# Making the first chunk's normalised MLP tiles one filler later in a streaming encoder layer

## The chip, the cores and the metric

The kernel runs on one core of a Trainium2 chip. The metric is the device time of one execution in microseconds, the median over several runs. One execution was also recorded by the hardware profiler; its instructions, waits and transfers are the trace that is read below. Engines are named as in the profile: PE (matrix multiplication), DVE (vector engine), ACT (scalar engine), POOL (GpSimd) and SP, whose queue issues most of the transfers.

## The reference

One layer over 1024 prompt frames and 32 sample frames, 1056 columns in all, with a model width of 1024, in float32. What matters here is the order of its parts:

```
x = x + (sigmoid(ga) * (A @ w_attn_out) + sigmoid(gb) * (B @ w_conv_out)) @ w_mix_out
x = x + softmax((rms_norm(x, g_cross) @ w_cq) @ K_mem.T) @ V_mem @ w_co      # 4 heads of 64, 256 memory tokens
x = x + square(relu(rms_norm(x, g_mlp) @ w_up)) @ w_down                     # hidden width 4096
y = rms_norm(x, g_final)
```

`rms_norm` divides a frame by the root of the mean square over its 1024 features and multiplies with a gain per feature.

## The kernel before

**Layout.** Features lie on the 128 partitions in eight blocks (f = 0 to 7), frames along the free axis. The 1056 frames are cut into three chunks of 384, 384 and 288 columns (`CH`, line 23). Every float32 operand of a matmul is split into a high and a low part (`split`, lines 128 to 130: ACT casts, DVE subtracts), and a product is three matmuls, high by high, high by low, low by high (`gemm`, lines 195 to 202). A projection of one weight block is 8 x 3 = 24 matmuls into one accumulator in PSUM. There are three accumulators (`n_acc`, line 103; tag "acc"), used in turn, so a projection can start only when the result three before it has been read out.

**The stage.** The change lies where three chunks overlap: chunk 0 is done with cross-attention and waits for the MLP, chunk 1 goes through cross-attention, and chunk 2 through its trunk, the eight projections of `do_conv_out` and then the eight of `do_mix`. The trunk projections and the first MLP products are the *fillers*: a list of 48 pieces of PE work (lines 1716 to 1723). Fillers 0 to 7 are `do_conv_out(2, f)`, 8 and 9 the first two of `do_mix(2, f)`, 10 is the first MLP product of chunk 0 (`up_one(0, 0)`). Behind each filler the table `at`, filled by `then(i, ...)` (lines 1724 to 1766), hangs further steps:

- at filler 1, `chunk_stats(1)`: chunk 1's scale, summed by small matmuls (L232), a root and a correction step (L238 to L243), spread over 128 partitions by L251 on ACT and L252 on DVE and two matmuls (L253, L254), copied to R by L266;
- at filler 2, `do_cq` twice: chunk 1's queries, each a projection of 24 matmuls of 384 columns, read out by L1142 and split by L1146 (ACT) and L1147 (DVE);
- at fillers 3, 5, 7, 9, 11 and 12, the cross-attention of chunk 1, a unit for each of the four heads, in three parts that are staggered by one step: `scores` (L1173 on PE, then L1176, L1179, L1181 on DVE and L1178 on ACT), `turn` (transposes L1190, split by L129 and L130 into PTh and PTl) and `values` (L1209, read out by L1211, L1212). Scores have one place in PSUM, so the next unit's wait until L1178 has read the last one's;
- at fillers 0 to 3, two a filler, `normed(0, f)` (lines 1316 to 1330): chunk 0's tile f, multiplied with gain and scale by L1318 on DVE, written to DRAM by L1321 on SP's queue, and its first 264 columns split by L1329 on ACT and L1330 on DVE. The split tiles are read by filler 10 (L890 to L892); the written ones are read back at filler 18 (L1265) and later.

`do_conv_out(2, f)` (lines 1070 to 1083) loads a residual part by L1074, runs the 24 matmuls, reads the accumulator out by L1078 on DVE (called the *eviction* of f), adds the residual by L1079 (POOL, for f = 7 DVE) and splits the sum by L129 and L130 into the tiles M. `do_mix(2, f)` reads all eight pairs of M and is read out by L1093.

**What sets the order.** Temporary tiles of DVE's steps and of these loads share one ring of six buffers (`tmp`, tag "ct", lines 29 and 105). The fillers and `at` give the program's order; a scheduler then places the instructions of each engine, but keeps those that are marked with `pin` in program order among themselves. L1318 and L1330 are marked so. On the chip each engine takes its own list strictly in that order, and each instruction waits for its operands and for the buffer that it writes.

## Time and profile before

| | us |
|---|---|
| median of three runs | 1738.01 |
| the three runs | 1736.62, 1738.01, 1741.13 |
| the profiled execution | 1736.25 |
| its span, first to last instruction | 1734.5 |
| PE busy | 1721.6 |
| DVE busy | 1194.1 |
| ACT busy | 852.4 |
| the eight tiles of chunk 0: first and last L1318 | 966.8 to 989.5 |

A row of the timeline gives the start from the span's beginning, the duration, the engine, the line, the operation, the tile written and the tiles read, and the shapes; a bracket at the end gives how long the engine had been idle just before, and what ended the wait. A row of windows gives a stretch, its length, the busy time of the five engines with instruction counts, the clock granted to PE as a share of full speed, the share of the transfer engines and GB/s. The profiler shows matmuls as longer than their spacing, since one begins while the one before drains; the spacing is read from the starts.

### The profile page before, as it was taken

The page shows a single profiled execution, that of the slowest core. Times are in us where ns is not written, and L with a number is a line of the kernel's source. Part 1 is how long each engine was busy: PE and PEld are TensorE (multiplying, and loading weights), DVE is VectorE, ACT ScalarE, POOL GpSimd, SP SyncE. Part 2 cuts the span into 40 slices and gives each one's busy share as a digit, 9 for nine tenths or more (in the row PEclk, how much of TensorE's full clock was granted, in tenths as well). Part 3 has the DMA queues.
Part 4 walks back from the last instruction along what each step waited for, and adds up shares of the span by engine and source line. Part 5 has one row for each costly group of instructions (what it writes and reads, how often), then busy time and mean ns, then how long its engine had stood idle before and what let it go on. Part 6 is the DMA issues. An engine that isn't in the chain of part 4 may idle for free.

```text
span 1734.5 us, 32561 instructions
## 1 busy us (share of the span) xinstructions
PE 1721.6 (99%) x12238; PEld 1707.3 (98%) x12238; DVE 1194.1 (69%) x2279; ACT 852.4 (49%) x1664; POOL 596.2 (34%) x668
## 2 busy tenths in 40 slices
PE   9999999999999999999999999999999999999998
PEld 8999999999999999999999999999999999999998
DVE  7776776867766657556677788787666686545675
ACT  8653533535335324434556666764444563433443
POOL 0026366453643444452225242106555410000121
PEclk9999999999999999999999999999999999999999
DMA  4333344433445888866865667676666695555554
GB/s 187 101 128 121 125 134 136 130 133 131 148 142 197 292 291 282 302 227 227 279 223 197 222 227 257 225 265 208 220 222 215 218 323 181 194 186 173 191 171 161
DMA packets 179853, 346.60 MB, mean 200 GB/s; under 512 B 18656, under 2 KB 101248, under 8 KB 179568
## 3 DMA queue, kind: packets, MB, share of 16 engines
q1 hardware_dynamic: 163504, 290.07, 50.6%
q0 software_dynamic: 15568, 53.68, 8.8%
q8 instruction: 96, 1.57, 0.4%
q10 hardware_dynamic: 624, 0.77, 0.1%
q14 instruction: 61, 0.50, 0.1%
HBM read 250.73 MB, written 93.14 MB: 198 GB/s over the span
## 4 chain that ended last, share of the span: by engine, by line
PE 88%; DMA 5%; DVE 3%; ACT 1%; issue 1%; POOL 1%; SPq 1%; DVEq 0%; ACTq 0%; POOLq 0%
PE acc L200 12%; PE acc L202 12%; PE acc L201 12%; PE acc L890 6%; PE acc L891 6%; PE acc L892 6%; PE acc L1830 5%; PE acc L1829 5%; PE acc L1828 5%; PE pc L890 2%; PE pc L891 2%; PE pc L892 2%; PE pt L607 2%; DVE wl L130 1%; DMA wr<-wsum_d 1%
## 5 line engine op out<-in xcount | busy, mean ns | idle before, releaser
L129 ACT CAST wh<-wr 128x1024 fp32r<-128x1024 f32 (+1 forms) x214 | 223.7, 1046 | 365.3 <-PE acc L1829 114.8
L130 DVE TENSOR_TENSOR wl<-wr,wh 128x1024 fp32r<-128x1024 f32 (+1 forms) x214 | 275.9, 1289 | 105.2 <-ACT wh L129 103.4
L200 PE MATMUL acc<-X,wh 128*128 128x384 f32 (+1 forms) x864 | 281.4, 326 | 0.0
L201 PE MATMUL acc<-X,wh 128*128 128x384 f32 (+1 forms) x864 | 278.5, 322 | 0.0
L202 PE MATMUL acc<-X,wl 128*128 128x384 f32 (+1 forms) x864 | 277.8, 322 | 0.0
L285 POOL TENSOR_TENSOR xacc<-xacc,ct 128x384 f32<-128x384 f32 (+1 forms) x57 | 77.7, 1366 | 380.8 <-ACT ct L283 379.0
L201 PEld LDWEIGHTS acc<-X,wh 128*128 128x128 f32 x864 | 162.7, 188 | 0.7
L200 PEld LDWEIGHTS acc<-X,wh 128*128 128x128 f32 x864 | 162.4, 188 | 0.8
L202 PEld LDWEIGHTS acc<-X,wl 128*128 128x128 f32 x864 | 162.4, 188 | 0.1
L200 PE MATMUL acc<-Y,wh 128*128 128x384 f32 (+1 forms) x432 | 139.8, 324 | 2.2 <-DVE ct L1078 2.2
L202 PE MATMUL acc<-Y,wl 128*128 128x384 f32 (+1 forms) x432 | 139.3, 323 | 0.1
L201 PE MATMUL acc<-Y,wh 128*128 128x384 f32 (+1 forms) x432 | 139.2, 322 | 0.0
L129 ACT CAST PTh<-pt 128x512 fp32r<-128x512 f32 (+3 forms) x94 | 45.8, 517 | 112.1 <-PE pt L607 110.4
L1828 PE MATMUL acc<-n,wh 128*128 128x264 f32 x352 | 100.2, 285 | 0.0
L1829 PE MATMUL acc<-n,wh 128*128 128x264 f32 x352 | 100.1, 284 | 0.0
L1830 PE MATMUL acc<-n,wl 128*128 128x264 f32 x352 | 100.0, 284 | 0.1
L744 POOL TENSOR_TENSOR ws<-ws 128x256 f32<-128x256 f32 x100 | 93.7, 937 | 5.7
L744 POOL TENSOR_TENSOR xacc<-xacc 128x256 f32<-128x256 f32 x100 | 86.5, 865 | 5.8 <-DMA xacc<-in_w_in 0.4
L200 PEld LDWEIGHTS acc<-Y,wh 128*128 128x128 f32 x432 | 81.1, 188 | 3.1 <-DVE ct L1078 3.1
L202 PEld LDWEIGHTS acc<-Y,wl 128*128 128x128 f32 x432 | 81.1, 188 | 0.4 <-DMA wl<-wl_d 0.4
L201 PEld LDWEIGHTS acc<-Y,wh 128*128 128x128 f32 x432 | 81.1, 188 | 0.0
L593 ACT ACTIVATE S<-S,nmx 128x257 f32<-128x257 f32 (+1 forms) x132 | 64.2, 488 | 20.1 <-DVE nmx L588 18.8
(440 smaller groups left out, 5555.3 us busy)
## 6 DMA issues: line engine op xcount, KB each, us to landing
wr<-in_w_up SPq DMA_DIRECT2D x53, 512.0 KB, 4.5
wr<-in_w_in SPq DMA_DIRECT2D x52, 512.0 KB, 3.6
wr<-wsum_d SPq DMA_DIRECT2D x40, 512.0 KB, 3.5
wr<-in_w_conv_out SPq DMA_DIRECT2D x24, 512.0 KB, 3.7
wr<-in_w_mix SPq DMA_DIRECT2D x24, 512.0 KB, 4.5
wr<-in_w_down SPq DMA_DIRECT2D x24, 512.0 KB, 3.6
n_d<-Z SPq DMA_DIRECT2D x32, 264.0 KB, 4.3
xacc<-in_w_down POOLq DMA_DIRECT2D x16, 512.0 KB, 4.6
```

The source lines that it names most:

```text
L129: act.copy(hi, src)
L130: dve.tensor_sub(lo, src, hi.bitcast(F32))
L200: pe.matmul(out, wh[:, a], hi, start=(k == 0), stop=False)
L201: pe.matmul(out, wh[:, a], lo, start=False, stop=False)
L202: pe.matmul(out, wl[:, a], hi, start=False, stop=(k == len(acts) - 1))
L744: pin(pool_e.tensor_tensor(t[:, to], t[:, x], t[:, y], op=ALU.add))
L890: pe.matmul(acc, wh[:, a], hi, start=(start and k == 0), stop=False, skip_group_check=True)
L891: pe.matmul(acc, wh[:, a], lo, start=False, stop=False, skip_group_check=True)
L892: pe.matmul(acc, wl[:, a], hi, start=False, stop=(k == 3), skip_group_check=True)
L1828: pe.matmul(a, wh[:, s], hi, start=(t == 0 and k == 0), stop=False, skip_group_check=True)
L1829: pe.matmul(a, wh[:, s], lo, start=False, stop=False, skip_group_check=True)
L1830: pe.matmul(a, wl[:, s], hi, start=False, stop=(t == 1 and k == 7), skip_group_check=True)
```

## The change

The loop that hangs the eight tiles behind the fillers starts at filler 1 instead of 0:

```
     for f in range(NF):
-        then(f // 2, call(normed, 0, f))
+        then(1 + f // 2, call(normed, 0, f))
```

Two tiles now come behind each of fillers 1 to 4. At filler 1 they stand behind `chunk_stats(1)`, at filler 2 behind the two query projections, at filler 3 ahead of the first scores, as the last two did before; filler 4 had nothing. The operations are the same; what the scheduler makes of them on each engine differs from about filler 1 to the end of the cross-attention of chunk 1.

The first place is DVE at the eviction of f = 1. In these names acc_11275 (after: acc_11261) is the accumulator of f = 1, ct_11253 and ct_11260 are the first two normalised tiles, wl is the low part of a weight. Before:

```order
L252 SCALAR_TENSOR_TENSOR ct_11243<-ident,rc_11225,ct_11242 128x128 x3
L130 TENSOR_TENSOR wl_11393<-wr_2080_11390,wh_11392 128x1024
L238 TENSOR_SCALAR st_v_11312<-pq_11308 128x3
L1318 SCALAR_TENSOR_TENSOR ct_11253<-Ga_1703_9819,prm,R_11240 128x384
L240 RECIPROCAL st_y_11314<-st_s_11313 128x3
L241 TENSOR_TENSOR st_t_11315<-st_v_11312,st_y_11314 128x3
L242 SCALAR_TENSOR_TENSOR st_t_11315<-st_t_11315,st_y_11314 128x3
L1330 TENSOR_TENSOR Y_2044_11257<-ct_11253,Y_2043_11256 128x264
L1318 SCALAR_TENSOR_TENSOR ct_11260<-Ga_1715_9868,prm,R_11240 128x384
L1078 TENSOR_TENSOR ct_11300<-acc_11275,Ga_1385_8179 128x288
```

and after:

```order
L252 SCALAR_TENSOR_TENSOR ct_11243<-ident,rc_11225,ct_11242 128x128
L1078 TENSOR_TENSOR ct_11286<-acc_11261,Ga_1385_8179 128x288
L252 SCALAR_TENSOR_TENSOR ct_11243<-ident,rc_11225,ct_11242 128x128 x2
L130 TENSOR_TENSOR wl_11379<-wr_2074_11376,wh_11378 128x1024
L238 TENSOR_SCALAR st_v_11298<-pq_11294 128x3
```

The eviction has moved from behind the weight split and the first two tiles into the group of L252 that spreads chunk 0's scale.

The second place is DVE at the evictions of f = 4 and f = 5 (acc_11563 and acc_11603 before, acc_11549 and acc_11603 after). S, rec and nmx belong to the softmax of a unit (unit 0: 11543 before and 11529 after; unit 1: 11642, nmx_11643; unit 2: 11757, nmx_11758; unit 3: nmx_11889). Before:

```order
L1179 RECIPROCAL rec_11546<-den_11545 128x3
L1181 TENSOR_SCALAR S_11543<-S_11543,rec_11546 128x256 x3
L130 TENSOR_TENSOR wl_11673<-wr_11670,wh_11672 128x1024
L1330 TENSOR_TENSOR Y_2110_11526<-ct_11522,Y_2109_11525 128x264
L1318 SCALAR_TENSOR_TENSOR ct_11529<-Gb_1786_10160,prm,R_11240 128x384
L1078 TENSOR_TENSOR ct_11588<-acc_11563,Gb_1481_8707 128x288
L1078 TENSOR_TENSOR ct_11628<-acc_11603,Gb_1516_8915 128x288
L1176 TENSOR_REDUCE nmx_11643<-sc_11635 128x3
```

After, the stretch that ends with the eviction of f = 4:

```order
L1176 TENSOR_REDUCE nmx_11643<-sc_11635 128x3
L130 TENSOR_TENSOR M_11505<-ct_11501,M_11504 128x288
L1318 SCALAR_TENSOR_TENSOR ct_11508<-Gb_1752_10017,prm,R_11240 128x384
L130 TENSOR_TENSOR PTl_11659<-pt_11654,PTh_11658 128x384
L130 TENSOR_TENSOR PTl_11667<-pt_11662,PTh_11666 128x384
L1179 RECIPROCAL rec_11645<-den_11644 128x3
L1181 TENSOR_SCALAR S_11642<-S_11642,rec_11645 128x256 x3
L1176 TENSOR_REDUCE nmx_11758<-sc_11750 128x3
L1330 TENSOR_TENSOR Y_2104_11512<-ct_11508,Y_2103_11511 128x264
L1318 SCALAR_TENSOR_TENSOR ct_11515<-Gb_1764_10066,prm,R_11240 128x384
L1078 TENSOR_TENSOR ct_11574<-acc_11549,Gb_1481_8707 128x288
```

and the later one that ends with the eviction of f = 5:

```order
L1181 TENSOR_SCALAR S_11757<-S_11757,rec_11760 128x256 x3
L130 TENSOR_TENSOR M_11578<-ct_11574,M_11577 128x288
L1318 SCALAR_TENSOR_TENSOR ct_11581<-Gb_1775_10113,prm,R_11240 128x384
L1176 TENSOR_REDUCE nmx_11889<-sc_11881 128x3
L130 TENSOR_TENSOR wl_11802<-wr_11799,wh_11801 128x1024
L1330 TENSOR_TENSOR Y_2123_11585<-ct_11581,Y_2122_11584 128x264
L1318 SCALAR_TENSOR_TENSOR ct_11588<-Gb_1786_10160,prm,R_11240 128x384
L1078 TENSOR_TENSOR ct_11628<-acc_11603,Gb_1516_8915 128x288
```

Before, the two evictions follow each other and stand ahead of unit 1's maximum; after, the first stands behind unit 2's maximum and the sixth tile (ct_11515), the second behind unit 3's maximum, a weight split and the last tile (ct_11588).

The third place is PE ahead of the projection f = 7 (acc_11718). pt_11654 and pt_11662 are the transposes of unit 0, pt_11783 and pt_11791 those of unit 1, o_11773 the values of unit 0. Before:

```order
L1173 MATMUL sc_11635<-mkl_9881,Y_2086_11426 128x256
L1190 MATMUL pt_11654<-ident,S_11543 128x128
L1190 MATMUL pt_11662<-ident,S_11543 128x128
L1190 MATMUL pt_11654<-ident,S_11543 128x128
L1190 MATMUL pt_11662<-ident,S_11543 128x128
L1190 MATMUL pt_11654<-ident,S_11543 128x128
L1190 MATMUL pt_11662<-ident,S_11543 128x128
L200 MATMUL acc_11718<-Y_1642_9578,wh_11597 128x288
```

and after:

```order
L1173 MATMUL sc_11750<-mkl_9930,Y_2086_11448 128x256
L1209 MATMUL o_11773<-PTl_11667,mv_10077 128x384
L1190 MATMUL pt_11783<-ident,S_11642 128x128
L1190 MATMUL pt_11791<-ident,S_11642 128x128
L1190 MATMUL pt_11783<-ident,S_11642 128x128
L1190 MATMUL pt_11791<-ident,S_11642 128x128
L1190 MATMUL pt_11783<-ident,S_11642 128x128
L1190 MATMUL pt_11791<-ident,S_11642 128x128
L200 MATMUL acc_11718<-Y_1642_9578,wh_11597 128x288
```

The values of unit 0, the scores of unit 2 and the transposes of unit 1, which stood behind f = 7 before, now stand ahead of it.

## The prediction

> **What bounds the kernel now.** I read the page first, then TensorE's waits, its timeline where those waits fall, and the vector engine's timeline at the same place. The page, and the answer on what PE waits for between 960 and 1040 us:

> ```profile
> span 1734.5 us, 32561 instructions
> PE 1721.6 (99%) x12238; PEld 1707.3 (98%) x12238; DVE 1194.1 (69%) x2279; ACT 852.4 (49%) x1664; POOL 596.2 (34%) x668
> PE acc L200 <- DVE ct L1078: 2.2, 3, 0.8
> ```

> PE is busy for all but 13 us of the span, so an edit that leaves PE's work alone can only remove or add waits of PE. In this stage nearly all of them have one cause: three times a projection cannot start because L1078 has not yet emptied one of the three accumulators. PE's rows at these places:

> ```profile
> 968.21 0.33 PE L202 MATMUL acc<-Y,wl 128*128 128x384 f32 x1
> 969.26 0.44 PE L200 MATMUL acc<-Y,wh 128*128 128x384 f32 x1 [0.72 <-DVE ct L1078]
> ...
> 973.71 0.34 PE L254 MATMUL pr<-ct,ones_r 128*128 128x384 f32 x1
> 974.89 0.40 PE L200 MATMUL acc<-Y,wh 128*128 128x288 f32 x1 [0.85 <-DVE ct L1078]
> ...
> 981.34 0.28 PE L1173 MATMUL sc<-mkh,Y 128*128 128x256 f32 x1
> ...
> 982.05 0.29 PE L200 MATMUL acc<-Y,wh 128*128 128x288 f32 x1
> ...
> 985.23 0.29 PE L200 MATMUL acc<-Y,wh 128*128 128x288 f32 x1
> ...
> 989.12 0.82 PE L1190 MATMUL pt<-ident,S 128*128 128x128 f32 x6
> 990.57 0.40 PE L200 MATMUL acc<-Y,wh 128*128 128x288 f32 x1 [0.63 <-DVE ct L1078]
> ...
> 995.21 0.34 PE L1209 MATMUL o<-PTl,mv 128*128 128x384 f32 x1
> 995.38 0.34 PE L1209 MATMUL o<-PTh,mv 128*128 128x384 f32 x1
> ```

> Matmuls overlap, so I count from start to start. A 384-column matmul takes 0.175 us of PE (4.2 for 24); the first gap is 1.05 - 0.18 = 0.87, the second 1.18 - 0.18 = 1.00, the third 1.45 less 0.66 for six transposes = 0.79; each restart costs 0.1 more. Together 2.97 us: the most that can be won here. A 24-matmul projection of chunk 2 takes 3.18 (982.05 to 985.23), six score matmuls 0.71, a values matmul 0.17.

> Whether DVE has room is in the windows of 1000 to 1020 us (PE, PEld, DVE, ACT, POOL busy; granted clock):

> ```profile
> 1000.00:1010.00 10.00, 10.00 (x81) 9.98 (x80) 9.72 (x21) 9.81 (x26) 3.08 (x3) 1.00 0.67 224
> 1010.00:1020.00 10.00, 10.00 (x79) 10.00 (x78) 9.94 (x18) 7.20 (x12) 4.63 (x4) 1.00 0.49 164
> ```

> DVE is 97 to 99% busy there: what is put later arrives where DVE is full.

> **The change part by part.** No operation is added or removed. I write N0 to N7 for the eight tiles; each is one L1318 and one L1330 on DVE, one L1329 on ACT, one write by L1321. Projection f of chunk 2 is "f0" to "f7", units 0 to 3 are the heads of chunk 1's cross-attention. What goes first: the evictions of f1 and f2 stood behind N0 to N3. DVE before:

> ```profile
> 959.68 0.16 DVE L238 TENSOR_SCALAR st_v<-pq 128x3 f32<-128x3 f32 x1 [0.33 <-PE pq L232]
> ...
> 961.48 0.94 DVE L252 SCALAR_TENSOR_TENSOR ct<-ident,rc,ct 128x128 fp32r<-128x128 f32 x3 [0.60 <-ACT ct L251]
> ...
> 966.38 0.16 DVE L238 TENSOR_SCALAR st_v<-pq 128x3 f32<-128x3 f32 x1 [0.80 <-PE pq L232]
> ...
> 968.23 0.61 DVE L1318 SCALAR_TENSOR_TENSOR ct<-Ga,prm,R 128x384 f32<-128x384 f32 x1
> 968.76 0.45 DVE L1078 TENSOR_TENSOR ct<-acc,Ga 128x288 f32<-128x288 f32 x1
> ...
> 977.97 2.31 DVE L1147 TENSOR_TENSOR Y<-ct,Y 64x384 fp32r<-64x384 f32 x4
> ...
> 980.85 1.22 DVE L130 TENSOR_TENSOR wl<-wr,wh 128x1024 fp32r<-128x1024 f32 x1
> 981.98 0.42 DVE L1330 TENSOR_TENSOR Y<-ct,Y 128x264 fp32r<-128x264 f32 x1
> 982.33 0.61 DVE L1318 SCALAR_TENSOR_TENSOR ct<-Gb,prm,R 128x384 f32<-128x384 f32 x1
> 982.86 0.45 DVE L1078 TENSOR_TENSOR ct<-acc,Gb 128x288 f32<-128x288 f32 x1
> 983.22 0.95 DVE L1176 TENSOR_REDUCE nmx<-sc 128x3 f32<-128x768 f32 x1
> ```

> The eviction of f1 starts at 968.76 without a wait of its own. In the new order it stands inside the first L252 group (about 962), so the first gap goes. Steps of DVE from start to start: weight split 1.13, L1330 0.35, L1318 0.53, L1078 0.36 (0.45 if last), L1176 0.87. To f2's eviction: L238 can start at about 966.2; from it to the end of L252 took 2.74 for chunk 0's scale; with the M split of f1 (0.4) that is 969.3, then N0, split, L1330, N1, eviction = 2.99, so 972.3. PE, not stopped, ends the second query projection and the broadcast at 968.4 + 4.2 + 0.35 = 972.9. The second gap goes too, and f3 starts at 972.9 instead of 974.89: 2.0 us ahead.

> What is added: N2 to N7 now fall among the attention units, and the new order of PE packs the units closer. Further steps:

> ```profile
> 987.05 0.18 DVE L1179 RECIPROCAL rec<-den 128x3 f32<-128x3 f32 x1 [0.38 <-ACT S L1178]
> 987.26 0.88 DVE L1181 TENSOR_SCALAR S<-S,rec 128x256 f32<-128x256 f32 x3
> ...
> 992.45 1.01 DVE L130 TENSOR_TENSOR PTl<-pt,PTh 128x384 fp32r<-128x384 f32 x2
> 993.38 0.44 DVE L1078 TENSOR_TENSOR ct<-acc,Gb 128x288 f32<-128x288 f32 x1
> ...
> 1000.60 0.44 DVE L130 TENSOR_TENSOR M<-ct,M 128x288 fp32r<-128x288 f32 x1
> 1000.97 0.55 DVE L1220 TENSOR_TENSOR Y<-tO,Y 64x384 fp32r<-64x384 f32 x1
> 1001.43 1.01 DVE L130 TENSOR_TENSOR PTl<-pt,PTh 128x384 fp32r<-128x384 f32 x2
> ```
> ```profile
> 985.55 0.47 ACT L1178 ACTIVATE S<-sc,nmx 128x256 f32<-128x256 f32 x1
> ...
> 990.50 0.85 ACT L129 CAST PTh<-pt 128x384 fp32r<-128x384 f32 x2
> ```
> ```profile
> L129 ACT CAST wh<-wr 128x1024 fp32r<-128x1024 f32 (+1 forms) x214 | 223.7, 1046 | 365.3 <-PE acc L1829 114.8
> L1079 POOL TENSOR_TENSOR ct<-ct,ct x7: 800/837/1004, 957.1 to 995.5; 128x288 f32<-128x288 f32 x7
> DMA to landing us min/median/max: 2.3/4.1/5.6
> ...
> L1330 DVE TENSOR_TENSOR Y<-ct,Y x8: 422/430/1035, 967.9 to 991.8; 128x264 fp32r<-128x264 f32 x8
> ```

> The landing time is that of L1074, the load that POOL's add waits for. Walking the new order with these steps (a walk by hand, an estimate from these rows):

> f6 needs f3's eviction. DVE ends the L1147 group at 980.28 as before, now with a weight split inside: 981.4; then N2, L1176 of unit 0, L1330, N3 and the eviction: 0.53 + 0.87 + 0.35 + 0.53 + 0.45, to 984.15. PE is done with f4, unit 0's scores and f5 at 972.9 + 9.54 + 0.71 = 983.15. A wait of 1.0; f6 is 1.1 ahead of its old 985.23.

> Unit 0's values. PE has 19 matmuls of f6, unit 1's scores, unit 0's transposes and only 5 more matmuls (0.66) before them; before, f7's whole 3.18 lay there. The transposes end at 988.1; DVE is at L1176 of unit 1 until 988.4, then M 0.37, N4 0.53, and the low part PTl until 989.85; PE could use it at 988.9: a wait of 1.0. Unit 2's scores then wait for ACT, which casts PTh until 989.1 and needs 3 x 0.47 for unit 1's exponentials: 0.25 more, start 990.5.

> f7 needs f4's eviction. After unit 2's scores, the last values matmul and unit 1's transposes PE is done at 992.05. DVE: L1179 and L1181 until 991.6, L1176 of unit 2 0.87, L1330 0.35, N5 0.53, eviction 0.45: 993.8. A wait of 1.75, where 0.79 stood.

> The first mix projection needs f5's eviction. PE: f7 3.18, unit 3's scores, unit 1's values, unit 2's transposes, done at 999.15. DVE after f4's eviction (step end 993.7): tO sum 0.47 (taken like L1220), PTl 0.93, L1179 0.21, L1330 0.35, L1220 0.46, L1181 0.80: 996.95. Then the M split of f4, which hangs on a load: SP issues it behind a weight load that waits for ACT's cast (991.6), so 992.0 + 4.1, POOL 0.84, ACT 0.43, M at 997.4 to 997.8. Then N6, L1176 of unit 3, weight split, L1330, N7, eviction: 0.53 + 0.87 + 1.13 + 0.35 + 0.53 + 0.45: 1001.65. A wait of 2.5, where none stood; queued behind that M split are all these, and PE waits for the last.

> From there I find none: both mix projections have 15 matmuls (4.0 us) ready, within which DVE ends N7 and f7's eviction (about 1004), and the 8 tiles are read only after them. The eight writes move on SP's queue with the tiles, past weight and residual loads; what reads them back stands at filler 18, after both mix projections and more, so I price the writes at nothing, and what they push back at the late load below.

> Sum: new 1.0 + 1.0 + 0.25 + 1.75 + 2.5 + four restarts of 0.1 = 6.9, less 2.97: **+3.9 us**. The profiled execution took 1736.25 (its span and 1.75 around it), so 1740.2; on the median of the three runs, 1738.01, 1741.9. Ends: +2.2 if DVE ends the L1147 group 1.0 earlier, half of what PE is ahead (f6's wait goes), and the load lands by 2.3 (0.7 less); +6.1 if it lands at 5.6 (1.5 more) and POOL's adds hold up DVE by the 0.6 that separates the median and the longest L1330 (a row of the same view). I take the median row for the load.

> [...] The two windows above show the clock at 1.00 behind waits of up to 1.0. [...]

> **The rivals.** (1) *DVE keeps up*: the gates are met and only the three old waits vanish, 1738.0 - 2.97 = 1735.0, or 1736.0 with the first two alone. For it: the rows above show DVE idle for 0.3 to 0.8 us at a time before, so some of its queue can slide. Against: it must be 1.75 and 2.5 us earlier than the walk at two gates, behind 97% of busy time. 20%.

> (2) *The late load* (the other side): f4's residual load, at its new place on SP, lands late; DVE stands at the M split with N6, N7 and f5's eviction behind it. It passes the bound of 0.3% (5.2 us of 1738.0, about what a measurement of this kernel can tell from no change) when it lands 1.3 us over the median, at 5.4; at 5.6 to 7 us it gives +5.4 to +6.8, up to 1744.8. 12%.

> [...] 3%.

> That the tiles are not moved is excluded by the order; a change elsewhere (a few rows differ after 1040 us) gets 5%.

> **How the numbers follow.** Forecast 60%, at 1741.9 with its own ends 1740.2 to 1744.1; about 7 points of it lie over +5.2. Slower: 7 + 12 + 3 + 1 = 23%. Faster by 5.2 is more than all waits of the stage; 3% for what I do not see. Within 0.3%: 74%. The range goes from 1736.5 (most of rival 1) to 1745.0 (most of rival 2).

> **What would show it.** Right: PE's wait at 969 and 974 gone; new waits of about 1.0 before f6 (L1078), 1.0 at L1209 (L130), 1.75 before f7 and 2.5 before the mix projection (both L1078), in all some 6 us of waits where the row of L1078 has 2.2. Wrong: DVE evicting f4 before 992 or f5 before 999; no wait at L1209; a wait at a matmul that reads the eight tiles; any difference that comes from outside this stage.

## The result, and the profile after

| | before | changed |
|---|---|---|
| median of six runs | 1738.70 us | 1747.39 us |
| lowest to highest | 1736.62 to 1741.13 | 1744.76 to 1751.71 |
| profiled execution, its span | 1736.25, 1734.5 | 1744.76, 1742.9 |

The changed kernel is slower: ratio 1.0055, 95% interval 1.0043 to 1.0067, 8.7 us by the medians, where +3.9 was forecast and 1745.0 was the upper end.

The page's first lines, and the answer on what PE waits for between 960 and 1040 us:

```profile
span 1742.9 us, 32561 instructions
PE 1724.8 (99%) x12238; PEld 1708.3 (98%) x12238; DVE 1191.2 (68%) x2279; ACT 852.9 (49%) x1664; POOL 597.2 (34%) x668
PE acc L200 <- DVE ct L1078: 3.6, 3, 2.1
PE o L1209 <- ACT PTh L129: 1.6, 1, 1.6
PE acc L200 <- DVE Gb L1093: 0.7, 1, 0.7
PE o L1209 <- DVE PTl L130: 0.7, 1, 0.7
```

PE was busy 3.2 us longer although it did the same 12238 matmuls. That is the first sign of something that is no wait. The places, in PE's timeline of the changed kernel:

```profile
973.90 0.40 PE L200 MATMUL acc<-Y,wh 128*128 128x288 f32 x1 [0.50 <-DVE ct L1078]
...
984.41 0.37 PE L200 MATMUL acc<-Y,wh 128*128 128x288 f32 x1
...
990.84 0.44 PE L1209 MATMUL o<-PTh,mv 128*128 128x384 f32 x1 [1.65 <-ACT PTh L129]
991.95 0.69 PE L1209 MATMUL o<-PTl,mv 128*128 128x384 f32 x1 [0.67 <-DVE PTl L130]
...
994.37 1.20 PE L1190 MATMUL pt<-ident,S 128*128 128x128 f32 x6
996.54 0.40 PE L200 MATMUL acc<-Y,wh 128*128 128x288 f32 x1 [0.97 <-DVE ct L1078]
...
1004.19 0.40 PE L200 MATMUL acc<-M,wh 128*128 128x288 f32 x1 [2.14 <-DVE ct L1078]
...
1006.03 0.44 PE L202 MATMUL acc<-M,wl 128*128 128x288 f32 x1
1006.27 0.44 PE L200 MATMUL acc<-M,wh 128*128 128x288 f32 x1
```

The first old wait is gone, a bracket of 0.50 is left of the second, and f3 starts 1.0 ahead of its old place. Then come the waits at unit 0's values (990.84, 991.95), before f7 (996.54) and before the mix projection (1004.19). The last two rows show the other thing: matmuls of 288 columns, 0.133 us apart otherwise, start 0.24 apart; and six transposes at 994.37 take 1.20 where they took 0.82. The granted clock is third from the end in the windows of this kernel:

```profile
988.38:991.79 3.41, 1.25 (x8) 0.76 (x6) 1.84 (x4) 1.81 (x6) 0.79 (x1) 0.99 0.89 265
991.79:995.20 3.41, 3.25 (x14) 3.02 (x15) 2.54 (x8) 2.48 (x7) 0.00 (x0) 0.51 0.55 202
995.20:998.61 3.41, 2.44 (x19) 2.21 (x18) 3.29 (x9) 3.06 (x11) 0.81 (x1) 1.00 0.52 187
...
1001.98:1005.39 3.41, 1.27 (x10) 1.20 (x10) 3.41 (x8) 2.93 (x10) 1.03 (x2) 1.00 0.84 252
1005.39:1008.80 3.41, 3.41 (x16) 3.41 (x16) 3.35 (x10) 1.30 (x4) 0.54 (x1) 0.50 0.51 168
...
```

(The columns: window, its length, busy time and instructions of PE, PEld, DVE, ACT and POOL, granted clock, DMA share, GB/s.) Twice the clock stands at one half for exactly one stretch of 3.41 us, and both times the stretch before held only 8 or 10 matmuls.

Where the time went: counted from start to start, the waits are 0.65 (f3), 0.17 (f6), 1.81 and 0.94 (values), 0.97 (f7, with the slow transposes taken out) and 2.29 (mix), and with 0.1 for each of four restarts 7.2 us (behind the wait at 973.90 the next matmul starts 0.24 later, where others of 288 columns stand 0.13 apart). The half-speed stretches add 3.25 / 2 + 3.41 / 2 = 3.3, an estimate from the granted clock of 0.51 and 0.50. Against the 2.97 of before that is +7.6. Just behind the stage PE waits 0.86 at 1026 and 0.44 at 1041 where it waited 0.34 before: +1.0. Together 8.6, where the spans differ by 8.4. The rest of the program comes out nearly even in sum only. Matmul for matmul, at times of the kernel before, the changed kernel is 0.3 us late at 955, 8.0 at 1015, 9.3 at 1040, 8.0 at 1080, 8.8 at 1160 and 8.5 at the end. It gains 1.3 between 1064 and 1080, where the kernel before has a half-speed stretch (its windows stand further down) and the changed one has none.

This tells where PE's time stood, not what each part would save. The first half-speed stretch is an example. A second profile of the changed kernel (run after_light, below) lacks it; there f7 waits 1.45 instead of 0.97, and the mix projection starts at 1004.06 instead of 1004.19, although f3 started 0.2 later. So that stretch, 1.6 by the sum above, delayed PE by about 0.3 net: without it PE comes earlier and waits for DVE instead.

The cause of the largest new wait stands in the timelines of the other engines. First the kernel before, then the changed one, around the residual load of f3 (L1074):

```profile
981.44 0.32 SPq L1074 DMA_DIRECT2D ct<-m_d  x1
981.82 0.45 SPq L172 DMA_DIRECT2D wl<-wl_d  x1
982.36 0.38 SPq L159 DMA_DIRECT2D wr<-in_w_mix  x1
982.84 0.38 SPq L159 DMA_DIRECT2D wr<-in_w_up  x1
...
984.34 0.84 POOL L1079 TENSOR_TENSOR ct<-ct,ct 128x288 f32<-128x288 f32 x1 [7.36 <-DMA ct<-m_d]
```
```profile
980.40 0.33 SPq L159 DMA_DIRECT2D wr<-in_w_mix  x1
980.82 0.38 SPq L172 DMA_DIRECT2D wl<-wl_d  x1
981.49 0.33 SPq L159 DMA_DIRECT2D wr<-in_w_up  x1
982.18 0.33 SPq L1321 DMA_DIRECT2D xn_d<-ct  x1
982.61 0.39 SPq L1074 DMA_DIRECT2D ct<-m_d  x1
...
989.15 0.79 POOL L1079 TENSOR_TENSOR ct<-ct,ct 128x288 f32<-128x288 f32 x1 [14.05 <-DMA ct<-m_d]
...
989.98 0.43 ACT L129 CAST M<-ct 128x288 fp32r<-128x288 f32 x1 [4.19 <-POOL ct L1079]
990.32 0.85 ACT L129 CAST PTh<-pt 128x384 fp32r<-128x384 f32 x2
991.06 0.49 ACT L1178 ACTIVATE S<-sc,nmx 128x256 f32<-128x256 f32 x1
...
990.44 0.46 DVE L130 TENSOR_TENSOR M<-ct,M 128x288 fp32r<-128x288 f32 x1 [1.57 <-ACT M L129]
```

Before, the load was issued ahead of three weight loads of 512 KB and let POOL start 2.9 us later; now it is issued 1.2 us later, behind three such loads and a write, and POOL starts 6.5 us after the issue. POOL's add waits for it, ACT's M cast waits for the add, and ACT takes its list in order: the PTh cast for unit 0 and the exponentials of unit 1, whose inputs were there at about 988.5 and 988.9, stand behind the M cast, for which ACT is idle 4.19 us. DVE stands the same way at the M split, idle for 1.57.

### The profile page after: what moved, and what is told of

It is laid out like the page before. It is cut to its first block, busy times and chain, and to the rows that moved or that the text cites. A ratio compares the mean times of both kernels' runs of the same rounds, so it can differ in the third digit from the quotient of the medians.

```text
span 1742.9 us, 32561 instructions
## 1 busy us (share of the span) xinstructions
PE 1724.8 (99%) x12238; PEld 1708.3 (98%) x12238; DVE 1191.2 (68%) x2279; ACT 852.9 (49%) x1664; POOL 597.2 (34%) x668
## 3 DMA queue, kind: packets, MB, share of 16 engines
q8 instruction: 96, 1.57, 0.4%
## 4 chain that ended last, share of the span: by engine, by line
PE 88%; DMA 5%; DVE 3%; ACT 2%; issue 1%; POOL 1%; SPq 0%; DVEq 0%; POOLq 0%; ACTq 0%
PE acc L200 12%; PE acc L202 12%; PE acc L201 12%; PE acc L890 6%; PE acc L891 6%; PE acc L892 6%; PE acc L1828 6%; PE acc L1830 6%; PE acc L1829 6%; PE pc L890 2%; PE pc L891 2%; PE pc L892 2%; PE pt L607 2%; DMA ct<-m_d 2%; DVE wl L130 1%
## 5 line engine op out<-in xcount | busy, mean ns | idle before, releaser
L129 ACT CAST wh<-wr 128x1024 fp32r<-128x1024 f32 (+1 forms) x214 | 223.7, 1046 | 367.4 <-PE acc L1829 124.3
L130 DVE TENSOR_TENSOR wl<-wr,wh 128x1024 fp32r<-128x1024 f32 (+1 forms) x214 | 276.8, 1294 | 108.3 <-ACT wh L129 107.3
L200 PE MATMUL acc<-X,wh 128*128 128x384 f32 (+1 forms) x864 | 281.4, 326 | 0.0
L202 PE MATMUL acc<-X,wl 128*128 128x384 f32 (+1 forms) x864 | 277.8, 322 | 0.0
L200 PEld LDWEIGHTS acc<-X,wh 128*128 128x128 f32 x864 | 162.4, 188 | 0.8
L202 PEld LDWEIGHTS acc<-X,wl 128*128 128x128 f32 x864 | 162.4, 188 | 0.1
L200 PE MATMUL acc<-Y,wh 128*128 128x384 f32 (+1 forms) x432 | 139.6, 324 | 1.5 <-DVE ct L1078 1.5
L202 PE MATMUL acc<-Y,wl 128*128 128x384 f32 (+1 forms) x432 | 139.2, 323 | 0.5 <-DMA wl<-wl_d 0.5
L129 ACT CAST PTh<-pt 128x512 fp32r<-128x512 f32 (+3 forms) x94 | 45.8, 518 | 113.1 <-PE pt L607 110.6
L1829 PE MATMUL acc<-n,wh 128*128 128x264 f32 x352 | 100.1, 284 | 0.0
L200 PEld LDWEIGHTS acc<-Y,wh 128*128 128x128 f32 x432 | 81.0, 188 | 2.2 <-DVE ct L1078 2.0
L202 PEld LDWEIGHTS acc<-Y,wl 128*128 128x128 f32 x432 | 81.1, 188 | 0.8 <-DMA wl<-wl_d 0.8
```

What stands on the lines that cost most here:

```text
L129: act.copy(hi, src)
L130: dve.tensor_sub(lo, src, hi.bitcast(F32))
L200: pe.matmul(out, wh[:, a], hi, start=(k == 0), stop=False)
L202: pe.matmul(out, wl[:, a], hi, start=False, stop=(k == len(acts) - 1))
L1829: pe.matmul(a, wh[:, s], lo, start=False, stop=False, skip_group_check=True)
```

## The experiments

My theory after reading this (theory 1 below): residual loads that land late hold ACT's and DVE's queues at the M split, PE waits for what is queued behind, and a stretch in which PE stood long enough costs half a stretch more. The rival (theory 2): DVE has too much to do, whatever the loads do. Ratios are to the kernel before, run on the same chip. An edit can shift the line numbers of a run's views: L1079 of one run can be L1080 of another, L1209 can be L1210 or L1214.

**The clock by itself.** A program of trains of matmuls, in which only a chain on DVE sets the wait between two trains. In short:

```
for count in (90, 100, 111):
    for width in range(0, 3072, 192):
        matmuls of 384 columns into g, count times
        t = g * 1e-4;  u = v[:, :width] * t[:, 0];  r = base * u[:, 0]   (DVE)
        the next train reads r
```

> This kernel leaves the whole computation out: it runs 48 trains of 90, 100 or 111 matmuls of 384 columns (about 16, 18 and 19 us), and between two trains PE waits for a chain on DVE that gets longer in 16 equal steps, the longest step 2880 columns more than the shortest. Theory 1 (fixed windows of 3.41 us, and a window in which PE stood for about half of it or more makes the next one run at half speed, as the three places in the two profiles suggest): waits of 1.3 us and less are never followed by a clock of 0.50; waits of 1.7 to 2.8 are followed by it in some trains and not in others, by where in a window they fall; waits of over 3.0 nearly always; each time for 3.4 us. [...]

Measured: 47 waits of 1.10 to 2.86 us; none of over 3.0, so that part of the expectation was not tried. Windows of 3.41 us in two places, 163.84 us or 48 steps of 3.413 us apart (PE, PEld, DVE ... granted clock):

```profile
416.97:420.38 3.41, 1.55 (x10) 1.23 (x9) 1.70 (x3) 0.00 (x0) 0.00 (x0) 1.00 0.00 0
420.38:423.79 3.41, 3.41 (x12) 3.41 (x11) 0.00 (x0) 0.00 (x0) 0.00 (x0) 0.50 0.00 0
...
580.81:584.22 3.41, 1.61 (x10) 1.28 (x8) 1.73 (x2) 0.00 (x0) 0.00 (x0) 1.00 0.00 0
584.22:587.63 3.41, 2.55 (x15) 2.56 (x16) 0.77 (x2) 0.00 (x0) 0.00 (x0) 1.00 0.00 0
```

The wait of 1.86 us, which lies in the first window whole, had 3.41 us at a clock of 0.50 behind it; that of 2.66, of which 1.80 lies in the window shown and 0.86 in another, had not. With all 47 waits laid on this grid of 3.413 us, the 20 with 1.86 or more in one window had half speed behind them, and the 27 with 1.80 or less had none. In PE's busy time, as these rows count it: 1.55 us of 3.41 with half speed behind it, 1.61 without. A wait of 2.46, cut into 1.13 and 1.33, cost nothing either: the 90 matmuls behind it took 15.87 us, as behind the shortest wait (15.90), where the 90 with one half-speed stretch among them took 17.44. Theory 1 holds here.

**The residual loaded elsewhere.** On the changed kernel and on before:

```diff
-            t1 = tmp(n)
+            mg[c][f] = (mslot(n), mslot(n))
+            t1 = mg[c][f][1].bitcast(F32) if c == 2 else tmp(n)
             sp.dma_start(t1, m1_d[c][:, f])
...
-            mg[c][f] = (mslot(n), mslot(n))
```

> The changed kernel, with the residual of chunk 2 loaded into the low half of the M slot that the split overwrites later, so that the load needs no tile of the ring of six; on SP's queue the load of projection f3 then stands ahead of the two weight loads that it stands behind in the changed kernel. Theory 1 (in the changed kernel f3's load, queued behind two 512 KB loads, lands at 989 and holds ACT, whose queue has the PTh cast of unit 0 behind the M cast): the wait of 1.65 at L1209 for L129 goes, PE waits under 1.0 there, the half-speed window behind it goes, and the time falls by 3 to 5 us, to a ratio of 1.002 to 1.004 over before. Theory 2 (DVE's queue alone is what is late; the load only fills time that would be lost anyway): ratio stays 1.005 to 1.006.

> The kernel before, with the same edit. Its load of f3 was in time already. Theory 1: within 2 us of before (ratio 0.999 to 1.001), the three waits of 0.6 to 0.9 at L200 for L1078 are still there. Theory 2 (loads matter nowhere in this stage): the same, so this run only shows that the edit by itself costs nothing.

Measured: 1741.04 us, ratio 1.0019 (1.0006 to 1.0033), and 1741.08, ratio 1.0012 (1.0002 to 1.0022). f3's load is issued at 974.37, ahead of the three weight loads, its add now starts at 985.82, and the wait for the PTh cast is gone. What PE waits for there in the changed kernel with the edit:

```profile
PE o L1209 <- DVE tO L1212: 1.8, 1, 1.8
PE acc L200 <- DVE ct L1079: 0.8, 1, 0.8
...
```

Six of the 8.7 us are gone, a little more than I had expected. With this edit in both, the two kernels take nearly the same time. But the scheduler also moved work behind f4, so this alone does not part the theories. On before the edit costs 2 us: the three old waits stay, and new ones come at 1009 to 1013.

**Parts of the change.** The line with `normed` has `then(f // 2 + (f >= 2), ...)` (six tiles later), `f // 2 + (f >= 6)` (two later), `max(1, f // 2)` (only the first two later), `f // 2 + (f >= 4)` (the last four later) and `4 + f // 2` (all four fillers later).

> The first two of the eight tiles at filler 0 as before, the other six one filler later as in the changed kernel. DVE's and PE's orders are then those of before up to the second query projection and those of the changed kernel behind f4. Theory 1 (the loss is made behind f4, the moves of the first tiles only win the first two waits): the gain of about 1.4 us is lost, but PE arrives later at the later waits, which shrink by as much; 1745 to 1749, ratio 1.004 to 1.006, with waits at L1209 and before the first mix projection. Theory 2 (what costs is that all eight tiles slide): about half the loss, 1741 to 1744.

> The kernel before with only the last two of the eight tiles at a later filler. SP's queue has f3's load ahead of the weight loads, as before. Theory 1: no wait at L1209 for L129, the old waits at L200 stay, at most 1 us is new before the first mix projection; ratio 1.000 to 1.002. Theory 2 (each tile that slides behind f5 costs): ratio 1.002 to 1.003.

> Four tiles at filler 1, two at 2, two at 3: only the first two tiles are later than before. On SP's queue f3's load stands behind one mix load but ahead of the wl and up loads. Theory 1: no wait at L1209 for L129; the first old wait goes (the eviction of f1 is ahead of the tiles), 1.0 to 1.5 us are won; ratio 0.998 to 1.001. Theory 2 (any tile that slides costs at the later gates): 1.001 to 1.003.

> The first four tiles at fillers 0 and 1 as before, the last four at 3 and 4. On SP's queue f3's load stands behind one mix load, ahead of the wl and up loads. Theory 1: the load is in time, no wait at L1209 for L129, the first two old waits stay; ratio 0.999 to 1.002. Theory 2 (DVE's queue alone, the last tiles falling among the units): 1.003 to 1.005.

> The tiles at fillers 4 to 7, behind f3: on DVE the evictions of f1, f2 and f3 are ahead of all tiles, but on SP's queue f3's load stands behind the wl and up loads, as in the changed kernel. Theory 1: the first two old waits go, a wait of over 1 for f3's residual is there at the scores, transposes or values of unit 0 or 1; ratio 1.002 to 1.005. Theory 2 (DVE's order alone): the evictions are early, so ratio 0.998 to 1.001.

Measured: six later 1747.21, ratio 1.0047 (1.0029 to 1.0064), with the same waits as the changed kernel: 1.71 for PTh, 0.67 for PTl, 2.07 before the mix. Two later 1738.14, ratio 0.9999 (0.9987 to 1.0011). The first two later 1744.68, ratio 1.0043 (1.0029 to 1.0056): my expectation of up to 1.5 us won was wrong. The last four later 1742.40, ratio 1.0029 (1.0016 to 1.0042), over the range that theory 1 had given; all four fillers later 1744.69, ratio 1.0043 (1.0028 to 1.0059).

In "first two later" there is a single wait. DVE's timeline ahead of it:

```profile
968.76 0.16 DVE L238 TENSOR_SCALAR st_v<-pq 128x3 f32<-128x3 f32 x1 [0.63 <-PE pq L232]
971.23 0.46 DVE L130 TENSOR_TENSOR M<-ct,M 128x288 fp32r<-128x288 f32 x1 [2.31 <-ACT M L129]
971.60 0.17 DVE L240 RECIPROCAL st_y<-st_s 128x3 f32<-128x3 f32 x1
...
979.90 0.45 DVE L1078 TENSOR_TENSOR ct<-acc,Ga 128x288 f32<-128x288 f32 x1
```

The M split of f1, which waits for its residual (POOL's add starts at 969.93, released by the load), stands between the statistics' first step and the rest; the statistics slide by 2.3 us, then four tiles and two weight splits stand ahead of f2's eviction at 979.90, and PE waits 4.77 us, with two half-speed stretches. So it is the M split again, two residuals earlier. In "last four later" f3's load is early, as I had read it, and POOL adds f3's residual at 979.49. But f4's load, issued at 984.23 behind three weight loads and a write, lets POOL start only at 991.70, 7.5 us after its issue; ACT is idle 2.35 for f4's M cast and DVE 2.22 for its M split. In "all four later" the forecast number came out at another place than I had said: 0.46 for PTh, but 1.98 for a weight split and 1.37 for L1093 at 1017 to 1021, with two half-speed stretches. DVE's timeline there:

```profile
1017.90 0.46 DVE L1093 TENSOR_TENSOR Ga<-acc,ct 128x288 f32<-128x288 f32 x1 [2.19 <-DMA ct<-in_x]
```

L1093 itself adds a residual, that of the mix projection, and DVE is idle 2.19 us for its load, which stands behind three weight loads on SP's queue (1008.70 to 1010.19); the weight split that PE waits for next comes behind it in DVE's order, at 1019.37. So this too is a late load that holds an in-order queue, at a place that theory 1 had not named, and not DVE's crowding.

**Two loads cut short.** An edit that was to leave seven eighths out of the two weight loads ahead of f3's residual named tiles that do not exist under that number, so nothing was cut and this is the changed kernel run again.

> The changed kernel with every engine's order as it is, but seven eighths left out of the two 512 KB weight loads (one low half for the projection f6, one up weight) that stand ahead of f3's residual load on SP's queue. Theory 1 (the late load): the residual lands some 3 us earlier, at about 986, ACT's M cast no longer holds the exponentials of unit 1 and the PTh cast of unit 0; PE's waits at L1209 fall from 2.3 to about 1.0, the half-speed window behind them goes, and DVE, which waited 1.57 for the M cast, comes that much earlier to f4's eviction; the wait before the first mix projection stays at about 2. In all 3 to 4.5 us less than the changed kernel: ratio 1.0025 to 1.0035. Theory 2 (DVE's queue alone): ratio 1.0045 to 1.006.

Measured: 1746.15, ratio 1.0048 (1.0036 to 1.0060). It says nothing on the theories, but it repeats the waits in a second profile (1.72 for PTh, 0.67 for PTl, 1.45 before f7, 2.39 before the mix), with one half-speed stretch in the stage instead of two. That the waits at the values fell into two windows of this execution is an estimate of mine.

**Low halves on POOL.** `pin(dve.tensor_sub(lo, ...))` of L1330 becomes `pin(pool_e.tensor_tensor(lo, ..., op=ALU.subtract))`, on the changed kernel and on before.

> The changed kernel with L1330 of the eight tiles on POOL instead of DVE: DVE has 8 x 0.35 = 2.8 us less to do in the stage. Theory 1 (two of the three parts of the loss, the late load and the clock windows, are not DVE's): the waits before f7 and the mix projection shrink by up to 2 us together, the rest stays; ratio 1.002 to 1.005. Theory 2 (DVE's queue alone): nearly the whole loss goes, ratio 1.000 to 1.002.

> The kernel before, with L1330 of the eight tiles on POOL. Both theories: the three waits at L200 for L1078 (0.72, 0.85 and 0.63) shrink or go, since DVE has 2.8 us less ahead of the evictions, unless POOL's shared work with DVE slows both; ratio 0.998 to 1.000.

Measured: 1740.60, ratio 1.0020 (1.0007 to 1.0033), and 1740.83, ratio 1.0017 (1.0006 to 1.0028). POOL takes 0.76 for what took DVE 0.43. On the changed kernel this gives back most of the loss, but the order changed with it and f3's add starts at 986.48, so both theories can claim it. On before, 2.8 us less on DVE won nothing: a new wait of 2.12 came at a unit's scores (L1173 for L1178), and ACT's timeline shows the exponentials of L1178 standing behind an M cast that waits 5.51 us for POOL's add. In the kernel before, the L1330 at 970.68, which starts within POOL's add of 970.42, took DVE 1.03, and that add took 1.00 where those of 957.10 and 995.47 took 0.80. Less work on DVE is not by itself worth time here.

**Nobody waits for the residual.** The add takes the tile itself: `tensor_tensor(t, t, t, ...)` in place of `(t, t, t1, ...)`, for f3 alone, then for all eight projections of chunk 2 on both kernels.

> The changed kernel, in which POOL's add of projection f3 adds the tile to itself: the residual of that one projection is left out of the sum, its load is still issued where it was, behind the two weight loads, but nothing waits for it. Theory 1 (the late load holds POOL, ACT's M cast and what stands behind it): PE's wait at L1209 for L129 (1.65 to 1.72) goes or falls under 0.6, DVE comes earlier to the evictions of f4 and f5; ratio 1.001 to 1.003. Theory 2 (DVE's queue alone): the eviction waits stay, ratio 1.004 to 1.006.

> The changed kernel, in which the adds of all eight projections of chunk 2 add the tile to itself: chunk 2's residual is left out, the loads are still issued where they were, and nothing waits for them. Theory 1 (a residual that lands late holds POOL's add, ACT's M cast and DVE's M split, and the units' work stands behind these in both queues; with f3's taken away in the last run f4's did the same): PE's waits at L1209 fall under 1.0 each, ratio 0.998 to 1.001, within 2 us of the same edit on the kernel before. Theory 2 (DVE has too much to do whatever the loads do): waits for L1078 of over 1.5 remain before f7 or the mix projection; ratio 1.003 to 1.005, and 4 us or more over the same edit on the kernel before.

> The kernel before with the same edit (chunk 2's residual left out of the sum). Theory 1: the loads were in time, so little changes: ratio 0.998 to 1.001. Theory 2: the same.

Measured for f3 alone: 1742.67, ratio 1.0033 (1.0020 to 1.0046). The wait for PTh at unit 0 is gone, and another of 3.42 has come at L1209. Its cause, in the timelines of that run:

```profile
995.72 0.81 POOL L1080 TENSOR_TENSOR ct<-ct,ct 128x288 f32<-128x288 f32 x1 [9.02 <-DMA ct<-m_d]
...
996.56 0.43 ACT L129 CAST M<-ct 128x288 fp32r<-128x288 f32 x1 [2.98 <-POOL ct L1080]
...
997.03 0.46 DVE L130 TENSOR_TENSOR M<-ct,M 128x288 fp32r<-128x288 f32 x1 [2.28 <-ACT M L129]
...
999.98 0.54 DVE L1213 TENSOR_TENSOR tO<-o,tO 64x384 f32<-64x384 f32 x1
```

It is f4's residual now, with ACT idle for 2.98 and DVE for 2.28, and the sum tO, for which PE waits, behind the M split with a tile, a weight split and a reduction between. With all eight left out: the changed kernel 1739.88, ratio 1.0018 (1.0007 to 1.0028), the kernel before 1738.40, ratio 1.0003 (0.9993 to 1.0013). What PE waits for, first in the changed kernel without residuals, then in before:

```profile
PE o L1209 <- DVE tO L1212: 1.8, 1, 1.8
PE acc L200 <- DVE ct L1078: 0.8, 1, 0.8
...
```
```profile
PE acc L200 <- DVE ct L1078: 1.9, 3, 0.7
PE acc L890 <- DVE Gb L1240: 0.9, 1, 0.9
```

The two kernels were 8.7 us apart and are now 1.5 apart. So with nothing waiting for residuals most of the loss is gone. One wait of 1.84 for DVE stays, which theory 1 had not expected; what of the 1.5 us DVE's order alone costs is not shown.

**The queues set free.** The M split of chunk 2's first six tiles goes to POOL, behind its add; nothing is left out:

```diff
+            if c == 2 and f in (0, 1, 2, 3, 4, 5):
+                hi, lo = mg[c][f]
+                pool_e.tensor_copy(hi, t)
+                pool_e.tensor_tensor(lo, t, hi.bitcast(F32), op=ALU.subtract)
+            else:
+                split(*mg[c][f], t)
```

> The changed kernel with the split of chunk 2's first six M tiles (cast and difference) on POOL behind its add, so that a late residual holds POOL alone and no longer ACT's and DVE's queues; nothing is left out. Theory 1: the units' casts are not held; ratio 0.998 to 1.002. Theory 2: DVE is relieved of 6 x 0.37 = 2.2 us, two thirds of the loss stays: ratio 1.002 to 1.004.

> The kernel before with the same edit, as a candidate for a faster kernel. Theory 1: the evictions come 0.4 us earlier each and ACT is never held: ratio 0.998 to 1.000. Theory 2: the same, by DVE's relief.

Measured: 1739.22, ratio 1.0014 (1.0005 to 1.0024), and 1737.92, ratio 1.0004 (0.9994 to 1.0014). In the changed kernel with this edit f3's add is as late as without it: its load is issued at 984.11, and POOL starts 6.5 us later, 15.1 us behind the start of f3 (15.2 without the edit). The bracket of this row names the transposes, which the add does not read; of what it does read, the eviction had ended at 985.72, so it was the load. PE's two largest waits in the stage are these:

```profile
990.58 0.80 POOL L1079 TENSOR_TENSOR ct<-ct,ct 128x288 f32<-128x288 f32 x1 [11.48 <-PE pt L1195]
```
```profile
PE acc L200 <- DVE ct L1078: 0.9, 1, 0.9
PE o L1214 <- DVE PTl L130: 0.8, 1, 0.8
...
```

The residual is as late, and no wait for PTh is left. A late addition need not cost: what cost was that casts and splits of other work stood behind it on ACT and DVE.

**What these runs do not take out.** The edits changed more than the loads and the splits. In the changed kernel, its second profile and "six later", three of unit 0's four values matmuls and unit 2's scores stand ahead of f7 on PE; in the five versions of the changed kernel that lost less (the load in the slot, low halves on POOL, no residual for f3 or for all, the split on POOL) the scheduler put them behind f7's 24 matmuls, which give PE 3.2 us of work while PTh is made. So PE's order is a third explanation, and no run here holds it fixed while the residual comes early. Two things speak for the residuals all the same. In the changed kernel the PTh cast could have started at 988.5 and started at 990.32, behind the M cast, and that is nearly the whole wait of 1.81. And in every version that lost 0.29% or more DVE stands idle for 1.57 us or more at a split or a sum that waits for a residual, under different orders of PE: f3's (changed, six later), f1's (first two later), f4's (last four later, no residual for f3), that of the mix (all four later). Of the versions that lost 0.20% or less only the two with the low halves on POOL have DVE waiting as long for POOL's add (1.65 at a split, 2.68 at an eviction). No version here beats the kernel before.

## Why the prediction was wrong, point by point

**The old waits.** "The first gap goes" was right. "The second gap goes too" was half right: 0.65 of 1.00 is left, because f1's M split, which the walk took at 0.4, held DVE for 1.56 us while f1's residual was still on its way (POOL's add at 966.94).

**f6.** Forecast 1.0, measured 0.17: f3's eviction ended at 984.26 where the walk had 984.15, but PE came 1.1 later than forecast, at 984.24.

**Unit 0's values.** Forecast 1.0 for the low part alone; measured 1.81 for the high part and 0.94 for the low. This is the place where a step failed outright: I priced SP's order only at f4's load, took f3's M split at 0.37 without a wait, and did not see that f3's load had moved behind three loads of 512 KB. Both orders showed it. The M split waited for that load until 990.44 where the walk had 988.4, and ACT was idle 4.19. The 0.25 forecast for unit 2's scores did not come.

**f7 and the mix projection.** Forecast 1.75 and 2.5, measured 0.97 and 2.29. The price of the mix wait was right with its cause: f5's eviction at 1003.70 behind the M split of f4 (999.92) and the tiles N6 and N7.

**The sum of the waits** was therefore 6.9 forecast against 7.2 measured, and that is luck: errors cancelled, too much at f6 and f7, too little at the values and at f3. The wait before f7 is also as short as 0.97 only because PE came late from a half-speed stretch; without it, in the second profile, it is 1.45.

**The clock.** The forecast held the clock at 1.00, and that is the other step that failed, by the sum the larger one. It fell to 0.50 behind waits of 2.75 (values) and 2.29 (mix), and by that clock PE's matmuls took 3.3 us longer. Of the 4.6 us between the forecast and the sum by place, 3.3 are these stretches, 1.0 lies behind the stage, and 0.3 in the waits. The clock's net price is smaller: 0.3 for the first stretch, by the two profiles, and up to 1.7 (half of 3.41, an estimate) for the second, which no profile of the changed kernel lacks. The windows of 1000 to 1020 us that I had shown at 1.00 could not have told: they begin 9 us behind the last of the old waits, at 990.57, and the stretches at half speed of the changed kernel, at 991.79 and 1005.39, stand directly behind the windows with 8 and 10 matmuls. The 3% that stands third among the rivals was for a fall of the clock; no run shows the condition that it was tied to, and what the runs showed in its place is a clock of 0.50 behind waits of 2.29 and 2.75 us. The trace of before had the evidence in it, at a place that I had not looked at. Its windows there:

```profile
1064.57:1067.98 3.41, 2.17 (x11) 1.45 (x11) 2.75 (x7) 3.38 (x8) 0.00 (x0) 1.00 1.02 351
1067.98:1071.39 3.41, 3.41 (x18) 3.41 (x17) 2.92 (x7) 2.59 (x7) 0.00 (x0) 0.50 0.53 186
```

Eleven matmuls of 264 columns, 1.3 us of work at 0.12 each, in one window, no single wait over 1.2, and the next window ran at half speed. (PE's busy time of 2.17 takes each row at its length, 0.28 to 0.40 for a single matmul there, where neighbours start 0.12 apart, so a count of matmuls is the safer reading here.)

**Behind the stage.** "From there I find none" left out +1.0: L1093 at 1026 and L1240 at 1041. And the changed kernel gained 1.3 at 1064 to 1080 and lost 0.8 by 1160, outside what the forecast looked at.

**The rivals.** DVE did not keep up. The late load, given for f4, happened at f3 instead, and both its chance and its price were too low, since a late residual holds two queues and not only the evictions. The clock fell, behind waits of 2.29 and 2.75 us.

What stays open: how much of the loss belongs to PE's order, with the values and scores ahead of f7, and not to the late residual; what the second half-speed stretch costs net; and how much of the last 1.5 us belongs to DVE's order and how much to half-speed stretches that a wait may or may not have behind it. A run with every engine's order kept and only f3's load moved was not made, since the scheduler answers every such edit with another order.

## What to carry to other kernels

When an edit moves work on an engine, follow every load that moves on the issuing queue with it, and ask which instructions stand behind the one that will wait for the load: the price here was not the late result but the ready work queued behind it, on each engine that had a step of it (ACT idle for 4.19 us, DVE for 1.57). Price a wait of PE by what it does to its clock as well: here the waits of 2.75 and 2.29 us had 3.41 us at a clock of 0.51 and 0.50 behind them, by that clock up to 1.7 us more each, and 0.3 net where PE would have waited for another engine anyway. A small residual that is added by an idle engine can be split there too, so that its delay stays there; on the changed kernel this took the ratio from 1.0055 to 1.0014, on the kernel before it won nothing.

## What the runs showed of the hardware

**A small load behind large ones.** 144 KB behind three loads of 512 KB and a write of 192 KB on one queue let POOL start 6.5 us after the issue (7.5 in "last four later"); ahead of such loads, 2.9.
